# Loading sixty tiles two at a time by one two-run DMA, and counting VectorE's adds over a lap, in a kernel that subtracts a mean of four rows

## The chip, the cores and the metric

The kernel runs on one core of one Trainium2 chip. The metric is the time of one execution in device microseconds. The kernel before takes 1285.2 us (median).

## The reference

```python
B, S, D = 8, 4096, 2112          # float32
x_r = x.reshape(B, S // 4, 4, D)
pooled = x_r.mean(axis=2)
return x - np.repeat(pooled, 4, axis=1)
```

The input is 276.8 MB and so is the output. Four elements (16 bytes read, 16 written) take eleven operations: three adds, four multiplications and four additions. That is about one operation for three bytes moved, so the first question is what the DMA engines do.

## The kernel before

A tile is 128 groups of four rows, one group in each partition: 33,792 bytes a partition, 4.33 MB in all, 64 tiles. Six slots in SBUF form a ring. SyncE issues the loads, ScalarE the stores, VectorE computes in place. A load waits until the store of the slot's last content has landed; a store waits for VectorE.

```python
def reduce_tile(b, parity):
    rows = slots[b].rearrange("p (f d) -> p f d", f=STRIDE)
    s = s_ps if parity else s_sb              # sums: PSUM and SBUF in turns
    add = nc.vector.tensor_add(out=s[:], in0=rows[:, 0, :], in1=rows[:, 1, :])
    add._wait_ge(load_sems[b], 16)
    add.then_inc(load_sems[b], -16)
    add = nc.vector.tensor_add(out=s[:], in0=s[:], in1=rows[:, 2, :])
    add.wait_op(load_sems[b], 0, "sem-eq")
    add.then_inc(step_sem)
    add = nc.vector.tensor_add(out=s[:], in0=s[:], in1=rows[:, 3, :])
    add._wait_ge(step_sem, 1)
    add.then_inc(step_sem, -1)
    sub = nc.vector.scalar_tensor_tensor(out=rows, in0=<s broadcast over 4 rows>,
        scalar=-1.0 / STRIDE, in1=rows, op0=mult, op1=add)
    sub.wait_op(step_sem, 0, "sem-eq")
    sub.then_inc(done_sem)
...
for k in range(n):                            # n = 64, SLOTS = 6
    b, lap = k % SLOTS, k // SLOTS
    load = nc.sync.dma_start(out=slots[b][:], in_=xg[k * P:(k + 1) * P])
    if lap:
        load._wait_ge(store_sems[b], 16 * lap)
    load.then_inc(load_sems[b], 16)
... # VectorE: 10 laps of a loop over six slots, then the last four tiles
for k in range(n):
    store = nc.scalar.dma_start(out=og[k * P:(k + 1) * P], in_=slots[b][:])   # b = k % SLOTS
    store._wait_ge(done_sem, k + 1)
    store.then_inc(store_sems[b], 16)
```

## Time and profile before

| | before |
|---|---|
| time, median (range) of 6 runs | 1285.20 us (1285.09 to 1285.26) |
| profile's span | 1283.3 us |
| DMA rate over the span | 431 GB/s |
| VectorE busy | 1026.5 us, 80% |
| one tile on VectorE | 16.04 us |
| one tile through the DMA engines, load and store | 19.97 us |

The last two rows are the whole argument: the engine with the longer time per tile sets the pace, as long as it always has work. The lines behind the table stand in the prediction, except the end of the kernel. It is in this part of the timeline (start, duration, engine, line, operation):

```profile
1188.58 80.21 ACTq L98 DMA_DIRECT2D out_dram<-slot  x5
1252.19 2.37 DVE L60 TENSOR_TENSOR s_ps<-slot 128x2112 f32<-128x2112 f32 x1 [3.78 <-DMA slot<-in_x_dram]
1259.46 8.96 DVE L69 SCALAR_TENSOR_TENSOR slot<-s_ps,slot 128x8448 f32<-128x8448 f32 x1
```

The first line merges the last five issues of stores; the last of them ends at 1188.58 + 80.21 = 1268.79. VectorE's last instruction ends at 1268.42, some 15 us before the span ends at 1283.3.

### The profile page before, as it was taken

The numbers are of one execution on the slowest core, as the hardware profiler recorded it, in microseconds if no ns is written. First come the engines' busy times: TensorE is split into PE (matmuls) and PEld (weight loads), VectorE is DVE, ScalarE is ACT, GpSimd is POOL, SyncE is SP. The second block draws the span as 40 slices with busy tenths as digits, with TensorE's granted clock in tenths as the row PEclk, the third lists the DMA queues.
The fourth block names the chain that finished last, engine by engine and source line by source line (L and its number), as shares of the span: only waits on it lengthen the run. The fifth ranks groups of instructions, "written<-read, shape, count | busy, mean of one in ns | idle before, by whom it ended". The sixth has DMA issues, their size and how long they took to land.

```text
span 1283.3 us, 591 instructions
## 1 busy us (share of the span) xinstructions
DVE 1026.5 (80%) x256; POOL 0.2 (0%) x4
## 2 busy tenths in 40 slices
DVE  5998788787787877878778787787887878878775
POOL 0000000000000000000000000000000000000000
DMA  9999999999999999999999999999999999999999
GB/s 404 421 437 433 428 438 432 428 438 437 431 430 438 432 428 438 437 429 432 438 432 428 438 436 429 433 438 432 428 438 435 429 434 438 432 428 438 434 427 404
DMA packets 18433, 553.66 MB, mean 431 GB/s; under 512 B 2048, under 2 KB 2048, under 8 KB 2048
## 3 DMA queue, kind: packets, MB, share of 16 engines
q1 hardware_dynamic: 9216, 276.83, 50.1%
q10 hardware_dynamic: 9216, 276.83, 50.0%
q14 instruction: 1, 0.01, 0.0%
HBM read 276.82 MB, written 276.82 MB: 431 GB/s over the span
## 4 chain that ended last, share of the span: by engine, by line
DVE 71%; another core or an unknown queue 23%; issue 3%; DMA 1%; DVEq 0%; SPq 0%
DVE slot L69 36%; DVE s_ps L66 6%; DVE s_ps L60 6%; DVE s_ps L63 6%; DVE s_sb L66 6%; DVE s_sb L63 6%; DVE s_sb L60 6%; DMA slot<-in_x_dram 1%; DVEq L66 0%; DVEq L60 0%; DVEq L90 0%; SPq L131 0%; SPq L82 0%
## 5 line engine op out<-in xcount | busy, mean ns | idle before, releaser
L69 DVE SCALAR_TENSOR_TENSOR slot<-s_sb,slot 128x8448 f32<-128x8448 f32 x32 | 286.6, 8957 | 1.1
L69 DVE SCALAR_TENSOR_TENSOR slot<-s_ps,slot 128x8448 f32<-128x8448 f32 x32 | 286.6, 8957 | 1.1
L60 DVE TENSOR_TENSOR s_sb<-slot 128x2112 f32<-128x2112 f32 x32 | 75.4, 2357 | 121.7 <-DMA slot<-in_x_dram 121.7
L60 DVE TENSOR_TENSOR s_ps<-slot 128x2112 f32<-128x2112 f32 x32 | 75.7, 2366 | 109.2 <-DMA slot<-in_x_dram 109.2
L66 DVE TENSOR_TENSOR s_ps<-s_ps,slot 128x2112 f32<-128x2112 f32 x32 | 75.7, 2367 | 3.3
L66 DVE TENSOR_TENSOR s_sb<-s_sb,slot 128x2112 f32<-128x2112 f32 x32 | 75.5, 2358 | 3.3
L63 DVE TENSOR_TENSOR s_ps<-s_ps,slot 128x2112 f32<-128x2112 f32 x32 | 75.7, 2366 | 1.1
L63 DVE TENSOR_TENSOR s_sb<-s_sb,slot 128x2112 f32<-128x2112 f32 x32 | 75.4, 2358 | 1.1
L120 POOL MEMSET const-bfloat16-1.0<- 128x1 bf16 x1 | 0.1, 102 | 0.0
L120 POOL MEMSET const-uint8-127<- 128x1 uint8 x1 | 0.1, 101 | 0.0
L120 POOL MEMSET const-float32-0.0<- 128x1 f32 x1 | 0.1, 99 | 0.2 <-issue 0.2
L120 POOL MEMSET const-float32-1.0<- 128x1 f32 x1 | 0.1, 98 | 0.0
## 6 DMA issues: line engine op xcount, KB each, us to landing
slot<-in_x_dram SPq DMA_DIRECT2D x64, 4224.0 KB, 59.7
out_dram<-slot ACTq DMA_DIRECT2D x64, 4224.0 KB, 43.7
```

The costliest lines, as they stand in the source:

```text
L60: add = nc.vector.tensor_add(out=s[:], in0=rows[:, 0, :], in1=rows[:, 1, :])
L63: add = nc.vector.tensor_add(out=s[:], in0=s[:], in1=rows[:, 2, :])
L66: add = nc.vector.tensor_add(out=s[:], in0=s[:], in1=rows[:, 3, :])
L69: sub = nc.vector.scalar_tensor_tensor(out=rows, in0=s[:, None, :].to_broadcast([P, STRIDE, D]), scalar=-1.0 / STRIDE, in1=rows, op0=mybir ...
L120: nc = _bacc.Bacc("TRN2", target_bir_lowering=False, num_devices=1)
```

## The change

One DMA loads two tiles, with two runs of 33,792 bytes in each partition, into two neighbouring slots: 30 pair loads, then four single ones. The intent is fewer and larger DMAs, and on VectorE a count over a whole lap in place of semaphores that go up and down at each tile. VectorE has still four instructions a tile.

```diff
-    slots = [io_pool.tile([P, W], f32, name=f"slot{b}") for b in range(SLOTS)]
+    ring = io_pool.tile([P, SLOTS * W], f32, name="ring")
+    slots = [ring[:, b * W:(b + 1) * W] for b in range(SLOTS)]
@@ reduce_tile @@
-        add._wait_ge(load_sems[b], 16)
-        add.then_inc(load_sems[b], -16)
-        ... (the second and third add, each with its own wait)
+        done = b * adds                       # adds = 3
+        for f in range(1, STRIDE):
+            first = rows[:, 0, :] if f == 1 else s[:]
+            add = nc.vector.tensor_add(out=s[:], in0=first, in1=rows[:, f, :])
+            if f == 1:
+                add._wait_ge(load_sem, landed)
+            else:
+                add._wait_ge(step_sem, done + f - 1)
+            add.then_inc(step_sem)
-        sub.wait_op(step_sem, 0, "sem-eq")
+        sub._wait_ge(step_sem, done + adds)
@@ loads @@
-        for k in range(n):
+        k = 0
+        while k < n:
+            size = 2 if k < PAIRED else 1     # PAIRED = 60
             b, lap = k % SLOTS, k // SLOTS
-            load = nc.sync.dma_start(out=slots[b][:], in_=xg[k * P:(k + 1) * P])
+            if lap and size == 2:
+                nc.sync.wait_ge(store_sems[b], 16 * lap)
+            load = nc.sync.dma_start(
+                out=ring[:, b * W:(b + size) * W].rearrange("p (j w) -> p j w", j=size),
+                in_=xg[k * P:(k + size) * P].rearrange("(j p) w -> p j w", j=size),
+            )
             if lap:
-                load._wait_ge(store_sems[b], 16 * lap)
+                load._wait_ge(store_sems[b + size - 1], 16 * lap)
             load.then_inc(load_sems[b], 16)
+            k += size
@@ VectorE's loop @@
-        with nc.vector.Fori(0, laps):
+        with nc.vector.Fori(0, laps) as lap:
+            landed = nc.vector.to_reg(16 * lap + 16)
             for b in range(SLOTS):
-                reduce_tile(b, b % 2)
+                reduce_tile(b, load_sems[b - b % 2], landed)
+            nc.vector.wait_ge(step_sem, SLOTS * adds).then_inc(step_sem, -SLOTS * adds)
```

More of the change, by code (lines that the diff above doesn't have):

```diff
@@ L10 @@
 SLOTS = 6
+PAIRED = 60
 PAD = 224
@@ L31 @@
     G = (B * S) // STRIDE
-    assert STRIDE == 4 and S % STRIDE == 0 and G % P == 0
+    assert S % STRIDE == 0 and G % P == 0
     n = G // P
@@ L53, with reduce_tile @@
     done_sem = tc.alloc_semaphore("done")
-    def reduce_tile(b, parity):
+    adds = STRIDE - 1
+    assert SLOTS % 2 == 0 and PAIRED % SLOTS == 0
+    def reduce_tile(b, load_sem, landed):
         rows = slots[b].rearrange("p (f d) -> p f d", f=STRIDE)
-        s = s_ps if parity else s_sb
-        add = nc.vector.tensor_add(out=s[:], in0=rows[:, 0, :], in1=rows[:, 1, :])
-        add._wait_ge(load_sems[b], 16)
-        add.then_inc(load_sems[b], -16)
-        add = nc.vector.tensor_add(out=s[:], in0=s[:], in1=rows[:, 2, :])
-        add.wait_op(load_sems[b], 0, "sem-eq")
-        add.then_inc(step_sem)
-        add = nc.vector.tensor_add(out=s[:], in0=s[:], in1=rows[:, 3, :])
-        add._wait_ge(step_sem, 1)
-        add.then_inc(step_sem, -1)
+        s = s_ps if b % 2 else s_sb
+        done = b * adds
[7 more added lines that the diff above has]
+            add.then_inc(step_sem)
         sub = nc.vector.scalar_tensor_tensor(
@@ L76, in reduce_tile @@
         )
-        sub.wait_op(step_sem, 0, "sem-eq")
+        sub._wait_ge(step_sem, done + adds)
         sub.then_inc(done_sem)
-    assert SLOTS % 2 == 0
     laps, rest = divmod(n, SLOTS)
+    assert laps * SLOTS == PAIRED
     with tc.tile_critical():
-        for k in range(n):
+        k = 0
+        while k < n:
+            size = 2 if k < PAIRED else 1
             b, lap = k % SLOTS, k // SLOTS
-            load = nc.sync.dma_start(out=slots[b][:], in_=xg[k * P:(k + 1) * P])
+            if lap and size == 2:
[4 more added lines that the diff above has]
+            )
             if lap:
-                load._wait_ge(store_sems[b], 16 * lap)
+                load._wait_ge(store_sems[b + size - 1], 16 * lap)
             load.then_inc(load_sems[b], 16)
-        with nc.vector.Fori(0, laps):
+            k += size
+        with nc.vector.Fori(0, laps) as lap:
+            landed = nc.vector.to_reg(16 * lap + 16)
             for b in range(SLOTS):
-                reduce_tile(b, b % 2)
+                reduce_tile(b, load_sems[b - b % 2], landed)
+            nc.vector.wait_ge(step_sem, SLOTS * adds).then_inc(step_sem, -SLOTS * adds)
         for b in range(rest):
-            reduce_tile(b, b % 2)
+            reduce_tile(b, load_sems[b], 16 * (len(range(b, n, SLOTS)) if b % 2 == 0 else 1))
         for k in range(n):
```

## The prediction

> **What bounds the kernel now.** I read the page first, and on it the row of the 40 slices, because the reference is one read and one write of every element with little arithmetic between.
>
> ```profile
> DVE 1026.5 (80%) x256; POOL 0.2 (0%) x4
> DMA  9999999999999999999999999999999999999999
> q1 hardware_dynamic: 9216, 276.83, 50.1%
> q10 hardware_dynamic: 9216, 276.83, 50.0%
> HBM read 276.82 MB, written 276.82 MB: 431 GB/s over the span
> ```
>
> The 16 DMA engines are busy in every slice, and the two queues' packets (q1 carries the loads, q10 the stores) together fill 100% of their time. VectorE is busy for 80%. The chain that ended last names VectorE for 71% of the span, which would mislead: the chain takes the last thing that released each step, and 23% of it is "another core or an unknown queue", that is, waits for data. So next I asked for the waits.
>
> ```profile
> DVE s_sb L60 <- DMA slot<-in_x_dram: 121.7, 30, 13.5
> DVE s_ps L60 <- DMA slot<-in_x_dram: 109.2, 29, 3.8
> ```
>
> VectorE waits for 59 of the 64 loads, about 3.8 us each (109.2 / 29): it has slack at every tile. Then I asked whether the rate depends on which queue has work: loads alone (before the first store), both, and the end.
>
> ```profile
> 5.00:30.00 25.00, 16.35 (x5) 0.00 (x0) 1.00 1.00 434
> 200.00:1200.00 1000.00, 803.93 (x202) 0.00 (x0) 1.00 1.00 433
> ```
>
> The last column is GB/s: 434 with loads alone, 433 with loads and stores. The rate belongs to the engines, not to the mixture. Last, the timeline near the end gives the period.
>
> ```profile
> 1192.27 2.36 DVE L60 TENSOR_TENSOR s_sb<-slot 128x2112 f32<-128x2112 f32 x1 [3.73 <-DMA slot<-in_x_dram]
> 1212.24 2.37 DVE L60 TENSOR_TENSOR s_ps<-slot 128x2112 f32<-128x2112 f32 x1 [3.76 <-DMA slot<-in_x_dram]
> 1232.20 2.36 DVE L60 TENSOR_TENSOR s_sb<-slot 128x2112 f32<-128x2112 f32 x1 [3.73 <-DMA slot<-in_x_dram]
> ```
>
> A tile begins every 19.97 us. In that time one load and one store of 4.33 MB go by, so one transfer takes 9.98 us of all 16 engines. 128 transfers are 1277.9 us. The chain of waits shows the first load from 0.95 to 13.37 us: 9.98 of transfer and 2.44 of fixed latency. So the transfers fill 3.4 to 1281.3 us, the last store's landing and the program's end take the other 2.0, and the sum is the span of 1283.3. Nothing is left over: the engines are never empty. The measured 1285.18 is 1.9 us above the profile's span.
>
> [...] with both queues full a tile passes each of them in 19.97 us, twice 9.98. [...]
>
> **The change part by part.** *Bytes and packets.* A pair load of 8.65 MB has two runs of 33,792 bytes in each partition, as long as the rows it replaces. Data packets stay 8,192 loads and 8,192 stores. 34 load DMAs in place of 64 remove 30 semaphore packets per engine. [...]
>
> *VectorE.* The three adds and the subtraction are the same instructions on the same shapes: 64 x 16.04 us. Per lap a register is computed and one wait added; ten times an estimated 0.1 to 0.2 us (the step between dependent adds is 0.1 us in the timeline), beside a slack of some 3.8 us a tile. On the path: 0.
>
> *The pair's later landing.* The first tile can start only when the second has landed: 13.37 + 9.98 = 23.35. VectorE takes 16.13 us a tile (13.47 to 29.60 in the timeline), so store 0 is issued near 39.6 instead of 29.71. This costs only if the engines run dry. Six slots of loads keep them busy until 3.4 + 6 x 9.98 = 63, so they don't.
>
> *The ring in steady state.* I follow it by hand with 9.98 alone, 19.97 shared. Loads run alone to about 42; pair 1 lands at 44.6, pair 2 two shared tiles later at 84.5. Stores 0 and 1 run from 42 to 82, which frees the first pair of slots at 82, before pair 2's load has ended: the load queue is just still full. Pair 3 lands at 124.4. Its tiles are done at 140.6 and 156.7, but stores 4 and 5 hold the queue until 162, so its stores run 162 to 182 and 182 to 202. From there all repeats every 39.93 us: a pair's load is issued about 2.4 us before the queue ahead of it is empty, and stores wait some 21 to 25 us in theirs. The load margin is thin, about one start-up latency. If the load queue does run dry, the stores take the freed turns at the full rate, finish sooner and release the next load sooner. No byte is lost as long as one queue has work.
>
> *The tail.* Pair 29 lands at 124.4 + 26 x 39.93 = 1162.6. The four single loads (issued at 1140, 1160, 1180, 1200, as stores 54 to 57 end) land at 1182.6, 1202.6, 1222.5 and 1242.5. VectorE, still behind by a pair, ends tile 60 at 1211, 61 at 1227, 62 at 1243.5, 63 at 1259.7. Stores 58 and 59 run to 1240.2, store 60 shares 2.3 us with the last load and ends at 1251.3, 61 at 1261.3, 62 at 1271.3, 63 at 1281.3. Store 63 is ready 11.6 us before its turn, so the engines are not idle at the end either, and the last transfer ends where it ends today.
>
> Sum: 1285.18 - 0.2 + 0 + 0 + 0 = 1285.0.
>
> **The rivals.** *The coarser ring starves the engines.* [...] both slots of a pair must be stored before the next load. For it: the thin load margin. Against: a pair needs 20 us of load alone, 32.3 of VectorE and about 10 more for its last store, some 62 to 65, where three pairs allow 120; the engines stop only if both queues are empty at once. If each lap lost 2.5 us it would be 25 us, 1310; a 10 us later start passed on to the end would make 1295.
>
> *Two runs are slower, or larger DMAs faster, per byte.* The alternation between two regions of HBM 4.33 MB apart could lower the rate. Against: each run is one 33 KB stretch, and reads and writes to far apart places already alternate at 433. If loads lost 5%, half the traffic, it would be 1285 + 32 = 1317. [...]
>
> *A transfer's turns change.* If an engine took two load packets for one of the stores', loads would land earlier and stores later; with no empty queue the end is the same, 1285.
>
> **Range and chances.** The result hangs on one fact, that some queue always has work, and the hand count has 10 us or more of margin at both ends. [...] a short gap at the start or the end pushes up by 1 or 2. So 1283.9 to 1286.8. [...] Slower by 2% (above 1310.9) needs a starved ring or slow runs: 0.02. The rest, 0.97, is within.
>
> **What would show it.** Right: the DMA row stays at 9 throughout and 433 GB/s; 480 semaphore packets vanish (30 x 16, so q1 has 8,736) and no others; VectorE's waits for loads come about once a pair, some 30 times and 7 to 8 us each (39.93 - 32.3), with the same total near 230 to 240; a store takes about 42 to 45 us to land (140.6 to 182, 156.7 to 202), a pair load about 42. Wrong: slices below 9 or below 430 GB/s in the middle (starving, or slow runs), a gap between the last VectorE instruction and the last store well under 20 us (tail bound by VectorE), or waits of VectorE that grow from pair to pair.

The sum came to 1285.0 us, that is 1285.18 less 0.2 for this term, which was my estimate and not shown. The low end of the range, 1283.9, rested on a larger figure for the same term; the 1 or 2 us for a gap, at the high end, were my allowance. The chance given to "faster by 2%" was 0.01.

The trace of the kernel before has these numbers. A semaphore packet took 9 ns, so 30 fewer on each engine are an estimated 0.27 us. Between 200 and 1200 us 6416 load packets and 6400 store packets started: the two queues shared the engines evenly. An add took 2358 ns (2366 with its sum in PSUM), the subtraction 8957. Stores alone, after the last load had landed at 1252.10, ran at 436 and 439 GB/s (1260 to 1270 and 1270 to 1280 us); and the window of e10 below in which the load queue restarted (610 to 640 us) has 435.

## The result, and the profile after

| | before | after |
|---|---|---|
| time, median (range), 6 runs each | 1285.20 us (1285.09 to 1285.26) | 1286.25 us (1284.77 to 1287.00) |
| ratio | | 1.0007, interval 0.9994 to 1.002 |

A ratio is the mean time of one kernel's runs over that of the other's of the same rounds, so not quite the ratio of the medians quoted. The medians differ by 1.05 us, and the changed kernel scatters over 2.2 us where the kernel before stays within 0.2.

The page of the changed kernel (its slowest run, 1287.0 us), the lines that answer to those of before:

```profile
DVE 1023.6 (80%) x256; POOL 0.2 (0%) x4
DMA  9999999999999999999999999999999999999999
q1 hardware_dynamic: 8736, 276.83, 50.1%
q10 hardware_dynamic: 9216, 276.83, 49.9%
HBM read 276.82 MB, written 276.82 MB: 431 GB/s over the span
```

The DMA row is full throughout, the bytes are the same, and q1 has lost 480 packets, the semaphore packets of 30 DMAs on 16 engines (4 bytes and 9 ns each in the records). The waits of VectorE, and then the mid-span rate from the view of windows (window, length, VectorE, GpSimd, clock, DMA share, GB/s):

```profile
DVE s_sb L68 <- DMA ring<-in_x_dram: 231.6, 28, 23.4
```

```profile
200.00:1200.00 1000.00, 802.40 (x202) 0.00 (x0) 1.00 1.00 434
```

The waits came half as often and twice as long: 28 times 8.3 us in place of 59 times 3.9 (without the first wait of each kernel, for the first load: 27 times 7.7 and 58 times 3.7). Their total moved from 230.9 to 231.6 us. The waits for the odd tile of each pair are gone, because it has landed with the even one. VectorE's idle time is what a bound elsewhere leaves over, and a coarser grain only deals it out in larger portions. The windows say why: 434 GB/s, as before.

The last load's issue, the last four stores' issues (merged) and VectorE's last instruction, in the timeline:

```profile
1202.78 0.33 SPq L94 DMA_DIRECT2D ring<-in_x_dram  x1
1213.62 48.52 ACTq L113 DMA_DIRECT2D out_dram<-ring  x4
1252.82 8.96 DVE L74 SCALAR_TENSOR_TENSOR ring<-s_ps,ring 128x8448 f32<-128x8448 f32 x1
```

VectorE ends at 1261.78, 23 us before the span's end at 1284.9. The last store stands in a queue, for 12.2 us (table of the tail below).

### The profile page after: what moved, and what is told of

It is laid out like the page before. It is cut to its first block, busy times and chain, and to the rows that moved or that the text cites. A ratio compares the mean times of both kernels' runs of the same rounds, so it can differ in the third digit from the quotient of the medians. Undisturbed runs are those within 1.5% of the kernel's fastest.

```text
span 1284.9 us, 480 instructions
## 1 busy us (share of the span) xinstructions
DVE 1023.6 (80%) x256; POOL 0.2 (0%) x4
## 4 chain that ended last, share of the span: by engine, by line
DMA 63%; DVE 34%; issue 1%; DVEq 0%; SPq 0%
DMA out_dram<-ring 32%; DMA ring<-in_x_dram 31%; DVE ring L74 19%; DVE s_sb L68 8%; DVE s_ps L68 8%; DVEq L103 0%; SPq L146 0%; SPq L87 0%
## 5 line engine op out<-in xcount | busy, mean ns | idle before, releaser
L74 DVE SCALAR_TENSOR_TENSOR ring<-s_sb,ring 128x8448 f32<-128x8448 f32 x32 | 286.7, 8958 | 1.1
L74 DVE SCALAR_TENSOR_TENSOR ring<-s_ps,ring 128x8448 f32<-128x8448 f32 x32 | 286.6, 8957 | 1.1
L68 DVE TENSOR_TENSOR s_sb<-ring 128x2112 f32<-128x2112 f32 x32 | 75.4, 2357 | 231.6 <-DMA ring<-in_x_dram 231.6
L68 DVE TENSOR_TENSOR s_ps<-s_ps,ring 128x2112 f32<-128x2112 f32 x64 | 151.4, 2366 | 2.2
L68 DVE TENSOR_TENSOR s_sb<-s_sb,ring 128x2112 f32<-128x2112 f32 x64 | 150.9, 2358 | 2.2
L68 DVE TENSOR_TENSOR s_ps<-ring 128x2112 f32<-128x2112 f32 x32 | 75.5, 2359 | 0.0
## 6 DMA issues: line engine op xcount, KB each, us to landing
ring<-in_x_dram SPq DMA_DIRECT2D x30, 8448.0 KB, 42.5
ring<-in_x_dram SPq DMA_DIRECT2D x4, 4224.0 KB, 42.5
```

The costliest lines, as they stand in the source:

```text
L68: add = nc.vector.tensor_add(out=s[:], in0=first, in1=rows[:, f, :])
L74: sub = nc.vector.scalar_tensor_tensor(out=rows, in0=s[:, None, :].to_broadcast([P, STRIDE, D]), scalar=-1.0 / STRIDE, in1=rows, op0=mybir ...
```

## The experiments

Twelve kernels ran. Theory **A** is the prediction's: the 128 transfers at 9.98 us each fill the DMA engines, one queue always has work, and VectorE's order of work doesn't matter. Its rivals say that VectorE's new counting costs the microsecond (B), that pairs use up the slack (C), or that some part of the change has a cost of its own that another part hides. The second question is where the 1.05 us and the scatter come from. My first answer was **T1**. In the changed kernel's trace, the issue and the landing of some transfers (us, from the DMA records) are:

```
load of pair 2 (tiles 4, 5)    issued  1.94   landed  83.16
store of tile 1                issued 55.60   landed  84.42
load of pair 3 (tiles 6, 7)    issued 84.44   landed 128.32
```

The load queue was empty from 83.16 to 84.44, and 17 data packets near 80 to 100 us took over 1.3 us in place of the usual 1.251; such packets are called lengthened below. T1 says that this restart of the load queue is the lost microsecond.

### Each half of the change alone

`e1_count_only` has single loads and the new counting; `e2_pairs_only` has pair loads and the old semaphores (the second tile of a pair counts its adds on `step_sem`, as its load is not waited for).

```diff
 e1, against the changed kernel
-        while k < n:
-            size = 2 if k < PAIRED else 1
-            ... (the pair load)
+        for k in range(n):
+            load = nc.sync.dma_start(out=slots[b][:], in_=xg[k * P:(k + 1) * P])
-                reduce_tile(b, load_sems[b - b % 2], landed)
+                reduce_tile(b, load_sems[b], landed)
 e2, against the changed kernel
-        with nc.vector.Fori(0, laps) as lap:
-            landed = nc.vector.to_reg(16 * lap + 16)
+        with nc.vector.Fori(0, laps):
-                reduce_tile(b, load_sems[b - b % 2], landed)
+                reduce_tile(b, None if b % 2 else load_sems[b])
```

> Half of the change: VectorE counts its adds over a lap, loads stay single. Theory A (the 128 transfers at 9.98 us each fill the DMA engines, VectorE has 3.8 us of slack a tile): 1285.2 within 0.2, runs as close together as those of the kernel before (0.2 us). Rival B (the 1.0 us that the change lost lies in VectorE's register waits): 1286.2.

> The other half: pair loads, with the semaphore handling of the kernel before on VectorE. Theory A with its detail T1 (the load queue runs empty once, near 83 us, because pair 3 can be issued only at 84.4 us, and the restart lengthens packets by 0.5 to 1.5 us on each engine): about 1286.2, runs spread over 1 to 2 us as in the changed kernel. Rival B (VectorE's counting): 1285.2.

Measured, five runs each, before beside them 1285.25 (1285.02 to 1285.49): e1 1285.13 us (1284.77 to 1285.32), ratio 0.9998 (0.9985 to 1.0012); e2 1286.51 (1285.85 to 1287.69), ratio 1.0011 (0.9997 to 1.0024). The counting on VectorE is free. The scatter and the microsecond go with the pair loads; the slowest run of e1 is faster than the fastest of e2, though each alone is "same".

### Taking the restart away

`e3_first_lap_single` loads the first six tiles singly, `e4_pair3_single` only tiles 6 and 7.

```diff
 e3
-            size = 2 if k < PAIRED else 1
+            size = 2 if SLOTS <= k < PAIRED else 1
 e4
-            size = 2 if k < PAIRED else 1
+            size = 2 if k < PAIRED and k not in (SLOTS, SLOTS + 1) else 1
 (both: the first lap, or the first two, written out ahead of VectorE's loop, with constant counts)
```

> Pairs from lap 1 on, the first six tiles singly: the first store leaves at 29.7 us as before, and the load queue does not run empty near 83 us. T1: 1285.2 within 0.3, spread under 0.4 us, no lengthened packets after 60 us. Rival T2 (the later first store, 39.5 us, is the loss): also 1285.2. Rival T3 (the 30 two-run DMAs themselves cost something): 1286.0 or more.

> The changed kernel with pair 3 alone (tiles 6 and 7) loaded singly: tile 6 can be issued at 65.7 us, when store 0 has landed, so the load queue stays full at 83 us; all else, the late first store too, stays. T1: 1285.2 to 1285.5 and spread under 0.5 us. T2 and T3: 1286.0 to 1286.3 with the spread of the changed kernel.

Measured: e3 1286.06 us (1285.24 to 1286.63), e4 1286.95 (1286.45 to 1287.50). Both miss T1's numbers. e4 was badly made: its trace has a load landing at 124.15 with the next pair issued at 125.44, so I had moved the empty moment and not removed it, and the lengthened packets moved with it: 39 between 100 and 140 us, none between 60 and 100. e3 has no empty load queue and, in its trace, two lengthened packets after 60 us. That trace is of a 1285.28 us run; three of the five runs were at 1286.06 to 1286.63 all the same. T2 falls with this, as the early store was back. T3 is not refuted by the median, but two of the five runs were at 1285.24 and 1285.28 with 27 pair loads in them; a fixed cost of each pair load would show in every run.

### A restart by itself

`e10_one_dry` and `e11_eight_dry` are the kernel before, in which one load, or eight, also waits for a store three tiles back, so that the load queue runs empty. `e12` is e3 once more.

```diff
 e10, against the kernel before (e11: range(14, 57, 6))
+            if k in (32,):
+                nc.sync.wait_ge(store_sems[(k - 3) % SLOTS], 16 * ((k - 3) // SLOTS + 1))
             load = nc.sync.dma_start(out=slots[b][:], in_=xg[k * P:(k + 1) * P])
```

> The kernel before, with one load (tile 32) held until store 29 has landed, so that the load queue runs empty once for some 10 us while stores go on. T1 (a restart of an empty load queue lengthens packets by 0.5 to 1.5 us on each engine, and nothing gives it back): 1285.7 to 1286.7, with lengthened packets near 660 us and nowhere else after 60. Rival (a restart costs nothing, the pairs' 1 us is of another origin): 1285.2, spread 0.4.

> The same at eight tiles (14, 20, ... 56). T1: eight times the cost of one restart, 1289 to 1294. Rival: 1285.2. Neither queue pair should be empty at once, so the engines' busy share should stay whole in both cases.

> The kernel with single loads in the first lap once more, as its five runs fell in two groups (1285.2 twice, 1286.1 to 1286.6 three times) and the trace was of a fast one. If the slower group is a property of pairs and not of that chip: again some runs near 1286.3. If the trace is of a slower one: late ends on some engines only, with lengthened packets in the middle of the span. T1 alone (only restarts cost) would give 1285.3 in all runs.

Measured: e10 1288.69 us (1288.59 to 1289.14), e11 1290.04 (1289.99 to 1293.18), e12 1286.14 (1285.01 to 1287.19), before 1285.10. e10 and e12 went against T1. e11 lies within T1's 1289 to 1294, but not for T1's reason, and e10 and e11 both went against its rival, that a restart costs nothing. e10 lost 3.6 us, more than T1 allows, yet its trace has no lengthened packet at the restart (613 to 623 us), and eight restarts cost not eight times as much but 4.9. The windows of e10 show where the time went: not around the restart or just after it (435 and 438 GB/s), but at the end:

```profile
610.00:640.00 30.00, 16.06 (x4) 0.00 (x0) 1.00 1.01 435
640.00:660.00 20.00, 13.01 (x4) 0.00 (x0) 1.00 1.01 438
1262.00:1270.00 8.00, 7.86 (x3) 0.00 (x0) 1.00 0.96 415
1270.00:1274.00 4.00, 4.00 (x1) 0.00 (x0) 1.00 0.28 118
1274.00:1278.00 4.00, 0.57 (x1) 0.00 (x0) 1.00 0.75 321
```

The same stretch of the kernel before:

```profile
1262.00:1270.00 8.00, 6.42 (x1) 0.00 (x0) 1.00 0.99 427
1270.00:1274.00 4.00, 0.00 (x0) 0.00 (x0) 1.00 1.04 448
```

In e10 the engines stand still around 1272: 4 x (1 - 118/433) + 4 x (1 - 321/433) = 3.9 us, about the loss. The hold at tile 32 left its mark on the order of the two queues for the remaining 600 us. In the issues view of 700 to 1200 us a load waits longer and a store shorter than the medians of before, 59.7 and 43.7:

```profile
slot<-in_x_dram SPq DMA_DIRECT2D x25, 4224.0 KB, 72.4
out_dram<-slot ACTq DMA_DIRECT2D x25, 4224.0 KB, 31.1
```

So the last tile lands later (1258.25 us, before 1252.10) and the earlier stores sooner (tile 60's at 1245.78, before 1252.26), while the store before the last lands as before (1272.38 and 1272.40). After it the engines have nothing to do and wait for VectorE. While both queues had work this shift cost nothing (433 GB/s from 700 to 1200 us); at the end it did. The loss of e10 lies at the tail, and that of e11 mostly (the table of the tail below).

### How much room VectorE has

`e5_one_more_add` and `e6_two_more_adds` do the first add once or twice more (the result is right).

```diff
-        for f in range(1, STRIDE):
+        for i in range(1, STRIDE + EXTRA):    # EXTRA = 1, 2
+            f = max(1, i - EXTRA)
```

> The changed kernel with the first add done twice (same result): VectorE takes 16.04 + 2.36 + 0.1 = 18.5 us a tile, still under the 19.97 us that a tile takes the DMA engines. Theory A: 1286 to 1289, the difference within 2 us of the changed kernel. Rival C (pairs have already used up VectorE's slack): 64 x 2.4 = 154 us more in the worst case, 1440, or some part of it.

> The first add three times: VectorE takes 16.13 + 2 x 2.41 = 20.95 us a tile, over the 19.97 us of the DMA engines. Theory A: VectorE becomes the bound, 23.4 + 64 x 20.95 + 12.4 + 1 = 1378 on the span, 1379 to 1381 us measured, DMA share under 95% in the middle. If it stays at 1286, VectorE's durations are not what bounds it and A's account is wrong.

Measured, before 1285.29: e5 1288.96 us (1288.85 to 1290.81), e6 1372.28 (1372.05 to 1372.32). e5's page:

```profile
DVE 1174.5 (91%) x320; POOL 0.2 (0%) x4
DMA  9999999999999999999999999999999999999997
```

150.9 us more work on VectorE (1174.5 - 1023.6) cost 2.7 us against the changed kernel's median, where I had expected at most 2. (The page and the trace are of e5's slowest run, 1290.81 us; the other three were at 1288.85 to 1289.00.) The last digit of the DMA row, 7, says where: VectorE ended after the store before the last had landed. In e6 the same two rows, and all of VectorE's waits for loads:

```profile
DVE 1323.5 (97%) x384; POOL 0.2 (0%) x4
DMA  9999999999999999999999999999999999999945
```

```profile
DVE s_sb L70 <- DMA ring<-in_x_dram: 23.2, 1, 23.2
```

A tile now takes 20.85 us on VectorE (20.83 and 20.87 in turn in its timeline), over the 19.97 of the DMA engines, and the bound has changed sides: VectorE waits once, for the first pair. 23.4 + 64 x 20.85 is 1357.8, the last store's 11.4 and the end's 1.0 make the span of 1370.1. My 1379 to 1381 had 20.95 a tile and was 6 us too high for that reason. The DMA share under 95% that I had also expected did not come:

```profile
200.00:1200.00 1000.00, 991.78 (x288) 0.00 (x0) 1.00 1.00 415
```

The share stays at 1.00 while the rate falls from 434 to 415 GB/s, because the packets took longer (1.295 us in the mean over the run, in place of 1.252 in the kernel before). So a DMA row of nines does not by itself say that the DMA engines set the pace; the GB/s and VectorE's waits tell it here. Theory A stands, and C falls: of some 3.9 us of room a tile, 2.4 more a tile still fit in e5, and the changed kernel's waits add up to what they did before (231.6 and 230.9 us).

### Grain against number of buffers

`e7_pairs_4_slots` has two buffers of two tiles, `e8_singles_4_slots` four of one (with the new counting), `e9_triples` two of three.

```diff
 e7, e8 (e8 against e1)
-SLOTS = 6
-PAIRED = 60
+SLOTS = 4
+PAIRED = 64
 e9
-            size = 2 if k < PAIRED else 1
+            size = 3 if k < PAIRED else 1
-                reduce_tile(b, load_sems[b - b % 2], landed)
+                reduce_tile(b, load_sems[b - b % 3], landed)
 (and one more wait of SyncE, for the store of the middle slot)
```

> Pairs in a ring of four slots, that is two buffers in place of three. Worked by hand with 9.98 us alone, 19.97 shared, 16.13 us of VectorE a tile, 2.4 us of latency: a pair takes some 46 us in place of 40, so 32 x 46 = 1470 (1420 to 1500), with stretches in which neither queue has work. If only the number of bytes counts: 1286. If only the number of slots counts, it equals the single loads over four slots.

> Single loads (VectorE counting over a lap) over the same four slots. By hand a slot needs about 20 + 16.1 + 20 us and twice 2.4 us of latency, 61 us of the 80 that four slots allow, and one queue always has work: 1286 to 1290. If the restart of an empty load queue costs 0.5 to 1.5 us each time and there is one a tile: 1320 to 1380. If four slots are too few whatever the grain: as the pairs over four slots.

> Three tiles in one load, six slots, so two buffers of three. By hand (9.98 alone, 19.97 shared, 16.13 of VectorE, 2.4 of latency): both queues are empty for a start-up latency at each hand-over, some 62 us per triple in place of 59.9, 21 triples, so about 1335. The run of pairs over four slots came out under its hand count (43 us a pair where I had 46), so 1310 to 1340. If only the number of buffers counts, two of them lose as much of the time as the two pairs over four slots did, 9%: 1400. If the number of slots counts: 1286.

Measured: e7 1400.67 us (1400.39 to 1400.76), e8 1289.74 (1289.50 to 1289.85), e9 1349.59 (1349.29 to 1352.04). Windows of e7, ten us each:

```profile
610.00:620.00 10.00, 0.00 (x0) 0.00 (x0) 1.00 1.00 433
620.00:630.00 10.00, 9.29 (x4) 0.00 (x0) 1.00 0.84 362
660.00:670.00 10.00, 7.36 (x4) 0.00 (x0) 1.00 1.00 433
670.00:680.00 10.00, 10.00 (x2) 0.00 (x0) 1.00 0.80 324
```

And of e9:

```profile
640.00:660.00 20.00, 6.35 (x3) 0.00 (x0) 1.00 1.00 433
660.00:670.00 10.00, 9.97 (x3) 0.00 (x0) 1.00 0.81 324
```

Within a hand-over the rate falls, once a pair, once a triple: the next load can be issued only when the last store of its buffer has landed, by then the other buffer's load has landed too, and nothing is in flight until the new load has started. The DMA records give the loss: on average an engine had no packet for 57 us at the hand-overs of e7, 1.8 at each of 31, and for 34 us in e9 (0.5 in the kernel before), and its packets took 43 and 27 us longer in sum. That makes 100 of the 115 us, and 61 of the 64. Nearly all the rest of e7's loss, 14 us, lies at its end, where the engines wait for VectorE before each of the last two stores. Pairs over three buffers don't come to this, because the third buffer's load is still in the queue (in the changed kernel a pair's load was issued at 244.19 us and the one ahead of it landed at 246.83).

My hand counts were 46 us a pair (43.2 in the trace) and 62 a triple (63.2), so e7 came out below its range and e9 above its. (The 21 triples of the expectation are 20, and four single tiles.) The direction and the mechanism were right; such a count by hand isn't good to 3% once the queues run empty.

Of e8's 4.5 us, 3.9 lie at the end of the kernel again (engines without a packet between 1260 and 1280 us). Its load queue ran empty once, at 54.4 us. The tail, from the DMA records and the issues (us):

| kernel | last store issued | store before it landed | wait in the queue | last store landed |
|---|---|---|---|---|
| before | 1268.45 | 1272.40 | 3.95 | 1282.36 |
| after | 1261.81 | 1273.99 | 12.2 | 1283.97 |
| e5, one more add | 1276.16 | 1273.79 | none, 2.4 late | 1287.51 |
| e8, singles over 4 slots | 1275.64 | 1274.41 | none, 1.2 late | 1286.98 |
| e10, one hold | 1274.60 | 1272.38 | none, 2.2 late | 1285.95 |
| e11, eight holds | 1275.60 | 1272.94 | none, 2.7 late | 1287.66 |

Where the last store stands in the queue it lands 9.96 to 9.98 us after the one before it. Where it comes late, it pays the lateness and its own start: 11.34 or 11.35 us from issue to landing (12.06 in e11). For e10 that is 2.2 + 11.35 - 9.96 = 3.6 us, the whole of its loss.

## Why the prediction was right

**The sum.** Predicted 1285.0, measured 1286.25, inside the range of 1283.9 to 1286.8; one run of six, 1287.00, was outside. The range reaches that far because of 1 or 2 us allowed for a gap at the start or the end. The surplus that came was of another kind (below), so that it was covered is in part luck. The sum's core, a pace set by 128 transfers with VectorE's work beside them, is shown by e5 and e6: 2.36 us more VectorE a tile changed the time only at the tail, twice that made VectorE the bound. The windows have 433 and 434 GB/s before and after.

**VectorE's counting, 0.** Shown by e1: 1285.13.

**The later first store, 0.** Store 0 was issued at 39.53 (predicted near 39.6), and e3, which restores the early store, has the same median as the changed kernel within 0.2 us.

**The start-up latency.** The prediction took the 2.44 us that the first load needed beyond 9.98 as a fixed latency. The records of the kernel before show where they went: the first packet started 1.0 us after the issue (0.95 to 1.95), the packets, eight on each engine, took 11.1 us from the first start to the last end in place of eight times 1.251, and the landing (13.37) came 0.3 us after the last of them.

**The ring.** The period was right (39.94 us). A pair's load was issued 2.6 us before the load ahead of it had landed (244.19 against 246.83; predicted 2.4), and stores took 39.9 and 45.1 us to land in turn (predicted 42 to 45), pair loads 42.5 (about 42). One step was wrong: "the load queue is just still full" at 82. I had left out a store's latency in that count; store 1 landed at 84.42 and the queue was empty for 1.3 us. That it would not matter much was also predicted, and the stores kept the engines at work (DMA share 0.99 from 80 to 100 us, at 409 GB/s with the lengthened packets).

**The tail.** 11.6 us of waiting were predicted for the last store, 12.2 measured. e5 used them up with its 14.4 us later VectorE and lost 2.7.

**The small term had the wrong sign.** I took 0.2 us off for 30 removed completions, an estimate that no trace had shown. Nothing of this is seen; in six slots, pairs cost 1.0 us (changed kernel) to 1.4 (e2 against e1) at the median. It is not a fixed cost of each pair load: the fastest runs with pairs, 1284.77 us (changed kernel) and 1285.01 (e12), are as fast as any of the kernel before. From the packet records, put in order for each of the 16 engines, the last data packets end between 1281.2 and 1281.9 us in the kernel before; in the changed kernel's slowest run twelve engines end between 1281.7 and 1282.0 and four between 1282.9 and 1283.5. The time is that of the latest engine, so a delay on a few of them is enough, and it scatters from run to run. In that trace the record also places the delay: near 98.5 us sixteen load packets, one on each engine, were lengthened at once, twelve of them to 1.70 to 1.85 us and four to 2.58 to 2.86. Counted over all packets after 60 us, lengthening comes to 0.8 us an engine here and in e2, to 1.0 in e4, and to 0.1 or less in the traces of before, e1, e3 and e12, all of them of runs at or below 1285.28.

What sets such a burst off is not settled. In the changed kernel, e2 and e4 most of it came 13 to 17 us after the restart, and e8, with single loads, has 31 lengthened packets at 62 to 71 us, after its load queue had run empty at 54.4. But e10's restart had none, e5's restart at 85.1 us had none in the 35 us after it, and e5 has a burst of 16 at 178 us without an empty load queue (a pair issued at 164.15, the one ahead landed at 166.66). So a restart is neither needed nor enough, and T1 as I put it falls. e3 and e12, which have no restart, still gave six runs of ten at 1286.06 to 1287.19, of which I have no trace. That the cost comes with pair loads in a ring of six slots is measured; its mechanism stays open.

**The rivals.** A starved ring was the right thing to fear and the wrong count: the load, compute and store times of a pair (62 to 65 us) stay under the 80 us of two buffers as well, yet e7 lost 9%. The mis-sized terms are the load and the store, taken at their times alone: in e7 a buffer's turn took 86 us, 34 for the load, 32 of VectorE and some 20 until the last store had landed. The condition that the prediction also names, that both queues are never empty at once, is the one that decided here (an engine was without a packet for 57 us at e7's hand-overs, for 0.5 us in the kernel before).

## What to carry to other kernels

Here the DMA engines were full (share 1.00 at 433 GB/s) and every row was already a long run (33,792 bytes), and fewer and larger DMAs gained nothing (1285.20 to 1286.25 us): look for a moment at which no queue has work, not at the number of DMAs. Count buffers at the grain of the transfers: two cost 5% and 9% here, while three of two tiles cost 0.1% and four of one tile 0.3%. (Three of one tile were not tried; the hand count of e8, 61 us a slot, would not fit into their 60.) And look at how long the last store waits in its queue: 4 us of slack there were invisible in the time, until a hold in the middle of the kernel used them up.
